# The mLSTM gates' eight columns, moved into the first memory query group

## The chip, the cores and the metric

The kernel runs on one core of a Trainium2 chip. The time is that of the device for one launch, in microseconds (us). Before the change it is 1012.1 us, the median of three runs (1011.96 to 1012.36). One further execution was recorded by the hardware profiler; every duration and start time below is from it.

The engines are TensorE (PE in the profile; PEld is its loading of stationary operands), VectorE (DVE), ScalarE (ACT), GpSimd (POOL) and SyncE (SP), whose queue issues the loads of weights. Each engine works through its own queue in order; semaphores tie the queues together.

## The reference, cut to what matters

The program is a decoder trunk of two layers for one sequence of 256 tokens with 1024 features. Layer 0 mixes tokens with an mLSTM, layer 1 with sliding-window attention; in both, four memory heads attend to 256 memory tokens. Each layer has a half-step SwiGLU feed-forward network before and after the mixing.

```python
hn = rms_norm(x, mix_norm_g[i])
proj = hn @ a_w_in[j]                       # 1024 x 3592
y_tok = mlstm_heads(proj[..., :A_TOK], a_gate_b[j], a_h_norm_g[j])
xq = proj[..., A_TOK:]                      # the 512 memory query columns
y_mem = memory_heads(xq, mem_k, mem_v, xa_q_norm_g[i], xa_k_norm_g[i])

# in mlstm_heads: q, k, v, the output gate, and then the eight gate columns
gates = tok[..., o4:].astype(f32) + gate_b.astype(f32)
i_pre = gates[..., :A_HEADS]                # 4 input gates
logf = jax.nn.log_sigmoid(gates[..., A_HEADS:])   # 4 forget gates
```

The forget gates are summed along the sequence, and a running maximum stabilises the exponentials. In the weight matrix, columns 3072 to 3079 are the gates, and columns 3080 to 3591 the memory queries: they lie next to each other.

## The kernel before, in words

All matrix products with weights are in fp32 split in two: a weight tile is loaded into `wr`, ScalarE casts it to a high part `wh` (L211), VectorE subtracts to get a low part `wl` (L212), and each product is three matmuls (`mm3`, L225 to L227): high by high, high by low, low by high. There are five `wr` buffers and eight of each of `wh` and `wl`, so the cast of a tile waits until TensorE is done with the tile eight before it. Activations are stored transposed (features in partitions) and split in `xh` and `xl` (L241), with the gain of the norm multiplied in; the norm's factor per token is applied to the products, as a row `rb` or as columns `rc`.

A `Group` (L316) makes 256 output columns: two weight tiles of four 128-row chunks, 24 matmuls each. With `rows=True` the activations are the stationary operand, and tokens come out in partitions; otherwise features do.

The order on TensorE and on SyncE's queue is the order in which the program emits the work. A small planner, `Weave`, decides that: one main chain emits groups, and side chains (`wv.spawn`) come in after a delay written in the table `LAT`, counted on a clock that the emitted matmuls advance. On VectorE, ScalarE and GpSimd the order is made when the program is built, by a scheduler; at run time they follow it strictly.

The mLSTM mixer (`mixer_a`, L649) emits in this order: four groups for the output gate (`g0`, `g1`, `g2` and a fourth); the gates; two groups of memory queries; groups for q and k; four groups for v; and the output projection. The gates before the change: the eight columns are loaded (L679) and put into columns 0 to 3 and 32 to 35 of a zeroed 128-column tile (L681 to L686), and eight `mm3` with this tile as stationary operand give the gates as rows in partitions 0 to 3 and 32 to 35 (L688 to L690). The gate chain on these rows (L693 to L708) is: copies out of PSUM, the product with `rb`, the bias, the log of a sigmoid (exp and ln on ScalarE), a sum scan, a maximum scan, and a last exp. The result `gg` is written to DRAM (L710), and read back twice, spread over all partitions, into `gb` (L713); both are issued from ScalarE's queue. 20 us after the gates on the planner's clock, `gate_cols` turns two of the rows into columns (`acol`).

`cross_spawn` (L568) handles a memory query group: `head_norm` (L368: square, sum, scaling, a power on GpSimd at L379, scaling, a product at L383), a side chain after `cross`, 9.5 us, that transposes the queries (`turn`, L387) and copies them out of PSUM to `qT` (L576, on ScalarE), and two heads, of which the first starts with the product of `qT` with `kT` (L588, recorded at L231). `scores` (L732) uses `gb` and `acol` for the mLSTM's own scores.

Of the kernel before, what the change touches and what calls it, by code (L numbers as in the profile page):

```python
# [10 lines left out]
F32 = mybir.dt.float32  # L11
# [8 lines left out]
P = 128  # L20
# [12 lines left out]
def constants():  # L33
# [17 lines left out]


LAT = dict(pieces=1, norm=7.5, norm_b=4.8, mnorm=2.4, x0=16.0, x0_b=7.5, mkeys=7.2, cross=9.5, cross_s=1.5,
           cross_m=3.7, cross_p=8.7, cross_o=3.0, gates=20.0, scores=2.2, scores_m=8.4, num=6.9, num_r=7.5,
           keys=5.5, keys_d=7.2, query=9.0, head=1.5, head_m=2.5, head_p=9.3, head_o=4.0)


# [41 lines left out]
def tile_trunk(ctx: ExitStack, tc: tile.TileContext, a, out):  # L99
# [31 lines left out]
    def act(*args, **kw):  # L131
        ins = nc.scalar.activation(*args, **kw)  # L132
        if args[2] not in (AF.Copy, AF.Square):
            tabled[0] = ins
# [232 lines left out]

    def head_norm(dst, src, n, hsc):  # L368

        hd = src.shape[2] // n  # L370
        sq, v, u = tmp(), col(), col()
        sqv = sq[:, :, :n * hd]
        act(sqv, src, AF.Square)
        nc.vector.tensor_reduce(out=v[:, 0:2 * n].rearrange("p (h m) -> p h m", h=2),
                                in_=sqv.rearrange("p h (m d) -> p h m d", m=n), axis=AX.X, op=ALU.add)
        for h in range(2):
            nc.vector.tensor_scalar(u[:, n * h:n * h + n], v[:, n * h:n * h + n], hsc[:, h:h + 1], EPS,
                                    op0=ALU.mult, op1=ALU.add)
        nc.gpsimd.tensor_tensor(out=u[:, 8:8 + 2 * n], in0=u[:, 0:2 * n], in1=mhalf[:, 0:2 * n], op=ALU.pow)  # L379
        for h in range(2):  # L380
            nc.vector.tensor_scalar(v[:, 8 + n * h:8 + n * h + n], u[:, 8 + n * h:8 + n * h + n],
                                    hsc[:, 2 + h:3 + h], None, op0=ALU.mult)
        tt(out=dst.rearrange("p h (m d) -> p h m d", m=n), in0=src.rearrange("p h (m d) -> p h m d", m=n),  # L383
           in1=v[:, 8:8 + 2 * n].rearrange("p (h m) -> p h m", h=2).unsqueeze(3).to_broadcast([P, 2, n, hd]),
           op=ALU.mult)
# [179 lines left out]
        def has(self, *kcs):  # L565
            return lambda: all(kc in self.done for kc in kcs)

    def cross_spawn(gr, gi, layer, hsc, ys):  # L568
        qn = unit(F32)
        head_norm(qn, gr.ps, 2, hsc)  # L570
        cell = []

        def queries():
            ps = turn(qn)
            qT = unit(F32)
            act(qT, ps, AF.Copy, scale=gqk[:, layer:layer + 1])  # L576
            cell.append(qT)
            for m in range(2):
                wv.spawn(head(m), LAT['cross_s'] + LAT['cross_m'] * m)
            return  # L580
            yield

        def head(m):
            hd, qT = gi * 2 + m, cell[0]
            hi, lo = ys.tiles(4 + gi)
            s = mo()
            for h in range(2):
                mmf(s[:, h * T:(h + 1) * T], qT[:, m, h * P:(h + 1) * P], kT[gi][:, m], T)  # L588
            sv = halves(s)
            c = col()  # L590
            nc.vector.tensor_reduce(out=c[:, 2:4], in_=sv, axis=AX.X, op=ALU.max, negate=True)  # L591
            p = unit(F32)
            for h in range(2):
                act(p[:, h], sv[:, h], AF.Exp, bias=c[:, 2 + h:3 + h], accum_out=c[:, 4 + h:5 + h])
            nc.vector.reciprocal(c[:, 6:8], c[:, 4:6])
            tt(out=p, in0=p, in1=c[:, 6:8].unsqueeze(2).to_broadcast([P, 2, T]), op=ALU.mult)
            yield LAT['cross_p']
            tps = mo()
            for mc in range(2):
                for h in range(2):  # L600
                    transpose(tps[:, mc * T + h * P:mc * T + (h + 1) * P], p[:, h, mc * P:(mc + 1) * P])
            pT = tmp()
            nc.scalar.copy(pT, halves(tps))
            yield LAT['cross_o']
            o = mo()
            for mc in range(2):
# [42 lines left out]
    def mixer_a(x, nxt):  # L649
# [25 lines left out]
        table("natural_log_exp_and_others")  # L675


        raw = mk(wrp, [P, 8, 8], F32, "wr")
        nc.sync.dma_start(raw, w.rearrange("(k p) f -> p k f", p=P)[:, :, 3072:3080])  # L679
        gh, gl = mk(whp, [P, 8, P], F32R, "wh"), mk(wlp, [P, 8, P], F32R, "wl")  # L680
        nc.vector.memset(gh.bitcast(F32), 0.0)  # L681
        nc.vector.memset(gl.bitcast(F32), 0.0)
        for s in range(2):
            src, dst = raw[:, :, s * 4:s * 4 + 4], slice(s * 32, s * 32 + 4)
            nc.scalar.copy(gh[:, :, dst], src)
            tt(out=gl[:, :, dst], in0=src, in1=gh[:, :, dst].bitcast(F32), op=ALU.subtract)  # L686
        ps = mo()
        for kc in range(8):  # L688
            mm3(ps[:, :T], gh[:, kc], gl[:, kc], x.xh[kc // 2][:, kc % 2], x.xl[kc // 2][:, kc % 2],
                start=kc == 0, stop=kc == 7)  # L690
        gt = [unit(F32) for _ in range(4)]
        ipre, fpre, ab, bc, av, gg, em, one = (gt[i // 2][0:4, i % 2] for i in range(8))
        nc.vector.memset(one, 1.0)  # L693
        nc.scalar.copy(ipre, ps[0:4, :T])
        nc.scalar.copy(fpre, ps[32:36, :T])
        tt(out=ipre, in0=ipre, in1=x.rb[0:4], op=ALU.mult)
        tt(out=fpre, in0=fpre, in1=x.rb[0:4], op=ALU.mult)
        nc.vector.tensor_scalar(ipre, ipre, gbias[:, 0:1], None, op0=ALU.add)
        nc.vector.tensor_scalar(fpre, fpre, gbias[:, 1:2], None, op0=ALU.add)
        nc.vector.scalar_tensor_tensor(out=ab, in0=fpre, scalar=-1.0, in1=fpre, op0=ALU.mult, op1=ALU.max)  # L700
        act(ab, ab, AF.Exp, scale=-1.0)
        act(ab, ab, AF.Ln, bias=1.0)
        nc.vector.scalar_tensor_tensor(out=fpre, in0=fpre, scalar=0.0, in1=ab, op0=ALU.min, op1=ALU.subtract)
        nc.vector.tensor_tensor_scan(bc, one, fpre, 0.0, ALU.mult, ALU.add)
        tt(out=av, in0=ipre, in1=bc, op=ALU.subtract)
        nc.vector.tensor_tensor_scan(gg, one, av, 0.0, ALU.mult, ALU.max)
        tt(out=em, in0=bc, in1=gg, op=ALU.add)
        act(em, em, AF.Exp, scale=-1.0)  # L708
        gd = a["gd"]
        nc.scalar.dma_start(gd, gg)  # L710
        gb = [unit(F32) for _ in range(2)]
        for i in range(2):
            nc.scalar.dma_start(gb[i], gd[2 * i:2 * i + 2, :].partition_broadcast(P))  # L713
        acol = mk(gp, [P, 16], F32, "acol")

        def gate_cols():
            pc = mo()
            for i, r in enumerate((av, em)):
                for h in range(2):
                    transpose(pc[:, (2 * i + h) * 4:(2 * i + h) * 4 + 4], r[:, h * P:(h + 1) * P])  # L720
            nc.vector.tensor_copy(acol, pc[:, :16])
            return
            yield

        wv.spawn(gate_cols(), LAT['gates'])
        hsc = head_scales(x.rc, P, True)
        for gi in range(2):
            gr = Group(w, 3080 + gi * 256, x.xh, x.xl, rows=True)
            yield from gr.all()
            cross_spawn(gr, gi, 0, hsc, ys)  # L730

        def scores(hd):  # L732
            row = gb[hd // 2][:, hd % 2]
            d = unit(F32).rearrange("p a b -> p (a b)")
            tt(out=d[:, :T], in0=maskd, in1=row, op=ALU.subtract)
            tt(out=d[:, T:384], in0=maskd[:, :P], in1=row[:, P:], op=ALU.subtract)
            act(d[:, :T], d[:, :T], AF.Exp, bias=acol[:, hd:hd + 1])
            act(d[:, T:384], d[:, T:384], AF.Exp, bias=acol[:, 4 + hd:5 + hd])
            q, k = qk[hd // 2][:, hd % 2], qk[2 + hd // 2][:, hd % 2]
            sps = mo()  # L740
            mmf(sps[:, :T], k[:, :P], q, T)
            mmf(sps[:, T:384], k[:, P:], q[:, P:], P)
            tt(out=d[:, :384], in0=d[:, :384], in1=sps[:, :384], op=ALU.mult)
            sd[hd] = d
            return
            yield

        for gi in (0, 2, 1, 3):
            gr = Group(w, gi * 256, x.xh, x.xl)
# [113 lines left out]
    def mixer_b(x, nxt):  # L863
# [26 lines left out]
                                  kn[:, :, :P].rearrange("p h (j d) -> p h j d", j=2))  # L890
        wv.spawn(keys(kdr, vr), LAT['keys'])
        hsx, hsq = head_scales(x.rc, P, True), head_scales(x.rc, 64, True)
        cross_spawn(g1, 0, 1, hsx, ys)
        gr = Group(w, 1280 + 256, x.xh, x.xl, rows=True)
        yield from gr.all()
        cross_spawn(gr, 1, 1, hsx, ys)

        def v22(x4):
            return x4.rearrange("p (h e) -> p h e", h=2)
# [127 lines left out]
```

## Time and profile before

| what | value |
|---|---|
| median of three runs | 1012.1 us (1011.96 to 1012.36) |
| the profiled execution | 1012.23 us |
| its span | 1010.4 us |
| TensorE busy | 998.5 us, 99% of the span |
| VectorE, ScalarE, GpSimd busy | 655.5, 519.5, 35.7 us |
| mean DMA rate | 181 GB/s |
| matmuls of the gates begin | 238.53 us |
| first memory group, second | 241.25 us, 246.69 us |
| first ScalarE copy of the gates (L694) | 242.51 us |
| write of `gg` to DRAM, issued | 249.36 us |
| first transpose of queries; first product with `kT` | 257.79 us, 260.96 us |

Times such as 242.51 us count from the start of the span. In a time line a row gives start, duration, engine, line, operation, what it writes and reads, and in brackets how long the engine was idle before and who ended that. Operations issued through helpers carry the helper's line: most ScalarE activations are L132. A matmul's duration overlaps the next; what one costs in a stream is the distance between starts.

### The profile page before, as it was taken

To read this page: it belongs to the slowest core of one execution; us is meant where nothing else is said; L and a number is where in the kernel's file an instruction comes from. 1 tells how busy PE (TensorE), PEld (TensorE's weight loads), DVE (VectorE), ACT (ScalarE), POOL (GpSimd) and SP (SyncE) were. 2 spreads that over 40 slices of the span, in tenths; PEclk is the share of its full clock that TensorE was granted. 3 is DMA by queue.
4 is the path that set the end of the run, shared out by engine and by line. 5 is a ranking of instruction groups with operands and counts; after the bars stand their busy time and mean duration, and the time that the engine had idled before them with its cause. 6 is when DMAs were issued, how large, how long until landed. Compare 5 with 4: busy or idle time off the path is not lost.

```text
span 1010.4 us, 20624 instructions
## 1 busy us (share of the span) xinstructions
PE 998.5 (99%) x8594; PEld 980.2 (97%) x8594; DVE 655.5 (65%) x1063; ACT 519.5 (51%) x764; POOL 35.7 (4%) x32
## 2 busy tenths in 40 slices
PE   8999999999999999999999999999999999999998
PEld 7999999999999999999999999999987899999998
DVE  6866665577856676665558666656787766666551
ACT  7754445446656554444445544544557754454440
POOL 1200000000001000000000000000121000000000
PEclk9999999999999999999999999999999999999999
DMA  9776656666644566665676666567541347666550
GB/s 308 242 245 200 192 180 185 199 183 179 184 139 133 167 210 195 200 189 170 192 206 205 189 191 201 173 197 198 182 131 66 100 131 220 198 189 185 188 170 21
DMA packets 173204, 182.70 MB, mean 181 GB/s; under 512 B 7124, under 2 KB 168328, under 8 KB 173112
## 3 DMA queue, kind: packets, MB, share of 16 engines
q1 hardware_dynamic: 171872, 179.60, 58.3%
q10 hardware_dynamic: 1016, 1.58, 0.5%
q8 instruction: 67, 1.10, 0.5%
q0 software_dynamic: 224, 0.22, 0.2%
q14 instruction: 25, 0.20, 0.1%
HBM read 180.32 MB, written 1.05 MB: 180 GB/s over the span
## 4 chain that ended last, share of the span: by engine, by line
PE 94%; DVE 3%; ACT 1%; DMA 1%; POOL 0%; issue 0%; SPq 0%; ACTq 0%
PE bank L225 30%; PE bank L226 30%; PE bank L227 30%; PE bank L231 2%; PE bank L236 1%; ACT u L132 1%; DVE wl L212 1%; DMA wr<-in_mem_w_kv_dram 1%; PE bank L961 1%; POOL col L379 0%; DVE col L930 0%; DVE u L383 0%; DVE col L591 0%; PE bank L925 0%; DVE u L946 0%
## 5 line engine op out<-in xcount | busy, mean ns | idle before, releaser
L212 DVE TENSOR_TENSOR wl<-wr,wh 128x1024 fp32r<-128x1024 f32 (+1 forms) x347 | 414.7, 1196 | 279.8 <-ACT wh L211 279.0
L211 ACT CAST wh<-wr 128x1024 fp32r<-128x1024 f32 (+1 forms) x347 | 356.8, 1031 | 393.1 <-PE bank L226 368.9
L225 PE MATMUL bank<-xh,wh 128*128 128x256 f32 x1544 | 429.1, 278 | 0.0
L226 PE MATMUL bank<-xl,wh 128*128 128x256 f32 x1544 | 426.8, 276 | 0.0
L227 PE MATMUL bank<-xh,wl 128*128 128x256 f32 x1544 | 426.8, 276 | 0.0
L226 PEld LDWEIGHTS bank<-xl,wh 128*128 128x128 f32 x1544 | 290.3, 188 | 0.1
L225 PEld LDWEIGHTS bank<-xh,wh 128*128 128x128 f32 x1544 | 290.0, 188 | 0.1
L227 PEld LDWEIGHTS bank<-xh,wl 128*128 128x128 f32 x1544 | 289.9, 188 | 0.0
L225 PE MATMUL bank<-u,wh 128*128 128x256 f32 x896 | 249.3, 278 | 0.0
L226 PE MATMUL bank<-u,wh 128*128 128x256 f32 x896 | 247.6, 276 | 0.0
L227 PE MATMUL bank<-u,wl 128*128 128x256 f32 x896 | 247.6, 276 | 0.0
L225 PEld LDWEIGHTS bank<-u,wh 128*128 128x128 f32 x896 | 168.2, 188 | 1.9 <-issue 1.7
L226 PEld LDWEIGHTS bank<-u,wh 128*128 128x128 f32 x896 | 168.4, 188 | 0.1
L227 PEld LDWEIGHTS bank<-u,wl 128*128 128x128 f32 x896 | 168.3, 188 | 0.0
L225 PE MATMUL bank<-wh,xh 128*128 128x256 f32 x208 | 59.7, 287 | 0.0
L226 PE MATMUL bank<-wl,xh 128*128 128x256 f32 x208 | 57.9, 278 | 0.0
L227 PE MATMUL bank<-wh,xl 128*128 128x256 f32 x208 | 57.9, 278 | 0.0
L476 DVE TENSOR_TENSOR t<-bank,rb 128x256 f32<-128x256 f32 x88 | 36.6, 420 | 7.3 <-PE bank L227 7.3
L225 PEld LDWEIGHTS bank<-wh,xh 128*128 128x128 f32 x208 | 39.1, 188 | 0.5 <-issue 0.3
L226 PEld LDWEIGHTS bank<-wl,xh 128*128 128x128 f32 x208 | 39.1, 188 | 0.1
L227 PEld LDWEIGHTS bank<-wh,xl 128*128 128x128 f32 x208 | 39.0, 187 | 0.0
L479 DVE TENSOR_TENSOR t<-t,bank 128x256 f32<-128x256 f32 x88 | 32.7, 412 | 1.8 <-ACT t L132 1.8
(171 smaller groups left out, 657.5 us busy)
## 6 DMA issues: line engine op xcount, KB each, us to landing
wr<-in_ffn_w_in_dram SPq DMA_DIRECT2D x176, 512.0 KB, 3.6
wr<-in_ffn_w_out_dram SPq DMA_DIRECT2D x80, 512.0 KB, 3.5
wr<-in_a_w_in_dram SPq DMA_DIRECT2D x28, 512.0 KB, 3.9
wr<-in_b_w_in_dram SPq DMA_DIRECT2D x14, 512.0 KB, 4.6
wr<-in_a_w_out_dram SPq DMA_DIRECT2D x12, 512.0 KB, 3.3
wr<-in_b_w_out_dram SPq DMA_DIRECT2D x12, 512.0 KB, 3.4
wr<-in_ffn_w_out_dram SPq DMA_DIRECT2D x16, 256.0 KB, 2.8
wr<-in_mem_w_kv_dram SPq DMA_DIRECT2D x7, 512.0 KB, 8.0
```

Source lines behind the costliest of these rows:

```text
L132: ins = nc.scalar.activation(*args, **kw)
L211: last[0] = nc.scalar.copy(hi[:, i * n:(i + 1) * n], src[:, i * n:(i + 1) * n])
L212: tt(out=lo[:, i * n:(i + 1) * n], in0=src[:, i * n:(i + 1) * n], in1=hi[:, i * n:(i + 1) * n].bitcast(F32), op=ALU.subtract)
L225: nc.tensor.matmul(ps, wh, xh, start=start, stop=False, skip_group_check=True)
L226: nc.tensor.matmul(ps, wh, xl, start=False, stop=False, skip_group_check=True)
L227: nc.tensor.matmul(ps, wl, xh, start=False, stop=stop, skip_group_check=True)
L231: nc.tensor.matmul(ps, lhsT, rhs, start=start, stop=stop, skip_group_check=True)
L236: nc.tensor.transpose(ps, src, ident[:k, :k])
L476: tt(out=t[:, m], in0=ps[m][:, :T], in1=x.rb, op=ALU.mult)
L479: tt(out=t[:, m], in0=t[:, m], in1=ps[m][:, T:], op=ALU.mult)
L961: nc.tensor.matmul(o[es[e], cs], vr[:, i, js], pTs[e][:, src], start=i == 0, stop=i == 1, skip_group_check=True)
```

## The change

The gates' eight columns and the first 256 memory query columns, neighbours in the weight matrix, are now one group of 264 columns. Its weights come in three tiles (3, 3 and 2 chunks of 128 rows, 264 columns wide), and the two halves of the tokens go to two PSUM banks. The gates come out with tokens in partitions; ScalarE scales them by `rc` into columns 0 to 3 and 32 to 35 of a zeroed buffer `gts`, and two transposes on TensorE turn them into the rows that the gate chain expects. The chain, now without the products with `rb`, and the DMAs of `gd` and `gb` are in a side chain `gates`, 1.8 us after the group on the planner's clock, and the transposes that make `acol` follow 13.5 us after that. `scores` puts itself off until `gated` is set. `head_norm` takes a list of two banks as well, and then does the square and the last product in halves.

```diff
-           ... gates=20.0, ...
+           ... gates=13.5, ... gate=1.8,
 def head_norm(dst, src, n, hsc):
...
+        if isinstance(src, list):
+            for h in range(2):
+                act(sqv[:, h], src[h], AF.Square)
...
+                tt(out=dst[:, h].rearrange("p (m d) -> p m d", m=n), in0=src[h].rearrange("p (m d) -> p m d", m=n),
+                   in1=v[:, 8 + n * h:8 + n * (h + 1)].unsqueeze(2).to_broadcast([P, n, hd]), op=ALU.mult)
...
-        raw = mk(wrp, [P, 8, 8], F32, "wr")
-        nc.sync.dma_start(raw, w.rearrange("(k p) f -> p k f", p=P)[:, :, 3072:3080])
-        gh, gl = mk(whp, [P, 8, P], F32R, "wh"), mk(wlp, [P, 8, P], F32R, "wl")
-        nc.vector.memset(gh.bitcast(F32), 0.0)
-        nc.vector.memset(gl.bitcast(F32), 0.0)
...
-        for kc in range(8):
-            mm3(ps[:, :T], gh[:, kc], gl[:, kc], x.xh[kc // 2][:, kc % 2], x.xl[kc // 2][:, kc % 2],
-                start=kc == 0, stop=kc == 7)
+        gts = unit(F32)[:, :, :36]
+        nc.vector.memset(gts, 0.0)
+        gps = [mo(), mo()]
+        for c0, nk in ((0, 3), (3, 3), (6, 2)):
+            wt = wtile(w.rearrange("(k p) f -> p k f", p=P)[:, c0:c0 + nk, 3072:3336], nk, 264)
+            for m in range(2):
+                ms = slice(m * P, (m + 1) * P)
+                for k in range(nk):
+                    kc = c0 + k
+                    mm3(gps[m][:, :264], x.xh[kc // 2][:, kc % 2, ms], x.xl[kc // 2][:, kc % 2, ms],
+                        wt[0][:, k], wt[1][:, k], start=kc == 0, stop=kc == 7)
+                yield
+        for h in range(2):
+            act(gts[:, h].rearrange("p (s c) -> p s c", c=4)[:, 0:9:8], gps[h][:, :8].rearrange("p (s c) -> p s c", s=2),
+                AF.Copy, scale=x.rc[:, h:h + 1])
...
-        tt(out=ipre, in0=ipre, in1=x.rb[0:4], op=ALU.mult)
-        tt(out=fpre, in0=fpre, in1=x.rb[0:4], op=ALU.mult)
...
+        gated = []
+
+        def gates():
+            ps = mo()
+            for h in range(2):
+                transpose(ps[:36, h * P:(h + 1) * P], gts[:, h])
...
+            nc.scalar.dma_start(gd, gg)
+            for i in range(2):
+                nc.scalar.dma_start(gb[i], gd[2 * i:2 * i + 2, :].partition_broadcast(P))
+            yield LAT['gates']
...
+            gated.append(True)
+
+        wv.spawn(gates(), LAT['gate'])
         hsc = head_scales(x.rc, P, True)
-        for gi in range(2):
-            gr = Group(w, 3080 + gi * 256, x.xh, x.xl, rows=True)
-            yield from gr.all()
-            cross_spawn(gr, gi, 0, hsc, ys)
+        cross_spawn([p[:, 8:264] for p in gps], 0, 0, hsc, ys)
+        gr = Group(w, 3080 + 256, x.xh, x.xl, rows=True)
+        yield from gr.all()
+        cross_spawn(gr.ps, 1, 0, hsc, ys)
 
         def scores(hd):
+            while not gated:
+                yield 1.0
```

More of the change, by code (lines that the diff above doesn't have):

```diff
@@ L53 @@
 LAT = dict(pieces=1, norm=7.5, norm_b=4.8, mnorm=2.4, x0=16.0, x0_b=7.5, mkeys=7.2, cross=9.5, cross_s=1.5,
-           cross_m=3.7, cross_p=8.7, cross_o=3.0, gates=20.0, scores=2.2, scores_m=8.4, num=6.9, num_r=7.5,
+           cross_m=3.7, cross_p=8.7, cross_o=3.0, gates=13.5, scores=2.2, scores_m=8.4, num=6.9, num_r=7.5, gate=1.8,
            keys=5.5, keys_d=7.2, query=9.0, head=1.5, head_m=2.5, head_p=9.3, head_o=4.0)
@@ L368, in head_norm @@
     def head_norm(dst, src, n, hsc):
-        hd = src.shape[2] // n
+        hd = dst.shape[2] // n
         sq, v, u = tmp(), col(), col()
         sqv = sq[:, :, :n * hd]
-        act(sqv, src, AF.Square)
+        if isinstance(src, list):
+            for h in range(2):
+                act(sqv[:, h], src[h], AF.Square)
+        else:
+            act(sqv, src, AF.Square)
         nc.vector.tensor_reduce(out=v[:, 0:2 * n].rearrange("p (h m) -> p h m", h=2),
@@ L382, in head_norm @@
                                     hsc[:, 2 + h:3 + h], None, op0=ALU.mult)
+        if isinstance(src, list):
+            for h in range(2):
+                tt(out=dst[:, h].rearrange("p (m d) -> p m d", m=n), in0=src[h].rearrange("p (m d) -> p m d", m=n),
+                   in1=v[:, 8 + n * h:8 + n * (h + 1)].unsqueeze(2).to_broadcast([P, n, hd]), op=ALU.mult)
+            return
         tt(out=dst.rearrange("p h (m d) -> p h m d", m=n), in0=src.rearrange("p h (m d) -> p h m d", m=n),
@@ L566, in has, with cross_spawn @@
             return lambda: all(kc in self.done for kc in kcs)
-    def cross_spawn(gr, gi, layer, hsc, ys):
+    def cross_spawn(ps, gi, layer, hsc, ys):
         qn = unit(F32)
-        head_norm(qn, gr.ps, 2, hsc)
+        head_norm(qn, ps, 2, hsc)
         cell = []
@@ L675, in mixer_a @@
         table("natural_log_exp_and_others")
-        raw = mk(wrp, [P, 8, 8], F32, "wr")
-        nc.sync.dma_start(raw, w.rearrange("(k p) f -> p k f", p=P)[:, :, 3072:3080])
-        gh, gl = mk(whp, [P, 8, P], F32R, "wh"), mk(wlp, [P, 8, P], F32R, "wl")
-        nc.vector.memset(gh.bitcast(F32), 0.0)
-        nc.vector.memset(gl.bitcast(F32), 0.0)
[L683 to L686, printed above, removed]
@@ L687, in mixer_a @@
-        ps = mo()
-        for kc in range(8):
-            mm3(ps[:, :T], gh[:, kc], gl[:, kc], x.xh[kc // 2][:, kc % 2], x.xl[kc // 2][:, kc % 2],
-                start=kc == 0, stop=kc == 7)
+        gts = unit(F32)[:, :, :36]
[10 more added lines that the diff above has]
+                yield
@@ L691, in mixer_a @@
+        for h in range(2):
+            act(gts[:, h].rearrange("p (s c) -> p s c", c=4)[:, 0:9:8], gps[h][:, :8].rearrange("p (s c) -> p s c", s=2),
+                AF.Copy, scale=x.rc[:, h:h + 1])
         gt = [unit(F32) for _ in range(4)]
         ipre, fpre, ab, bc, av, gg, em, one = (gt[i // 2][0:4, i % 2] for i in range(8))
-        nc.vector.memset(one, 1.0)
-        nc.scalar.copy(ipre, ps[0:4, :T])
-        nc.scalar.copy(fpre, ps[32:36, :T])
-        tt(out=ipre, in0=ipre, in1=x.rb[0:4], op=ALU.mult)
@@ L697, in mixer_a @@
-        tt(out=fpre, in0=fpre, in1=x.rb[0:4], op=ALU.mult)
[L698 to L708, printed above, removed]
         gd = a["gd"]
-        nc.scalar.dma_start(gd, gg)
         gb = [unit(F32) for _ in range(2)]
-        for i in range(2):
-            nc.scalar.dma_start(gb[i], gd[2 * i:2 * i + 2, :].partition_broadcast(P))
@@ L714, in mixer_a @@
         acol = mk(gp, [P, 16], F32, "acol")
-        def gate_cols():
+        gated = []
+        def gates():
+            ps = mo()
+            for h in range(2):
+                transpose(ps[:36, h * P:(h + 1) * P], gts[:, h])
+            nc.vector.memset(one, 1.0)
+            nc.scalar.copy(ipre, ps[0:4, :T])
+            nc.scalar.copy(fpre, ps[32:36, :T])
+            nc.vector.tensor_scalar(ipre, ipre, gbias[:, 0:1], None, op0=ALU.add)
+            nc.vector.tensor_scalar(fpre, fpre, gbias[:, 1:2], None, op0=ALU.add)
+            nc.vector.scalar_tensor_tensor(out=ab, in0=fpre, scalar=-1.0, in1=fpre, op0=ALU.mult, op1=ALU.max)
+            act(ab, ab, AF.Exp, scale=-1.0)
+            act(ab, ab, AF.Ln, bias=1.0)
+            nc.vector.scalar_tensor_tensor(out=fpre, in0=fpre, scalar=0.0, in1=ab, op0=ALU.min, op1=ALU.subtract)
+            nc.vector.tensor_tensor_scan(bc, one, fpre, 0.0, ALU.mult, ALU.add)
+            tt(out=av, in0=ipre, in1=bc, op=ALU.subtract)
+            nc.vector.tensor_tensor_scan(gg, one, av, 0.0, ALU.mult, ALU.max)
+            tt(out=em, in0=bc, in1=gg, op=ALU.add)
+            act(em, em, AF.Exp, scale=-1.0)
+            nc.scalar.dma_start(gd, gg)
+            for i in range(2):
+                nc.scalar.dma_start(gb[i], gd[2 * i:2 * i + 2, :].partition_broadcast(P))
+            yield LAT['gates']
@@ L721, in gate_cols @@
             nc.vector.tensor_copy(acol, pc[:, :16])
-            return
-            yield
-        wv.spawn(gate_cols(), LAT['gates'])
+            gated.append(True)
+        wv.spawn(gates(), LAT['gate'])
         hsc = head_scales(x.rc, P, True)
-        for gi in range(2):
-            gr = Group(w, 3080 + gi * 256, x.xh, x.xl, rows=True)
-            yield from gr.all()
-            cross_spawn(gr, gi, 0, hsc, ys)
+        cross_spawn([p[:, 8:264] for p in gps], 0, 0, hsc, ys)
+        gr = Group(w, 3080 + 256, x.xh, x.xl, rows=True)
+        yield from gr.all()
+        cross_spawn(gr.ps, 1, 0, hsc, ys)
         def scores(hd):
+            while not gated:
+                yield 1.0
             row = gb[hd // 2][:, hd % 2]
@@ L744, in scores @@
             sd[hd] = d
-            return
-            yield
         for gi in (0, 2, 1, 3):
@@ L892, in mixer_b @@
         hsx, hsq = head_scales(x.rc, P, True), head_scales(x.rc, 64, True)
-        cross_spawn(g1, 0, 1, hsx, ys)
+        cross_spawn(g1.ps, 0, 1, hsx, ys)
         gr = Group(w, 1280 + 256, x.xh, x.xl, rows=True)
         yield from gr.all()
-        cross_spawn(gr, 1, 1, hsx, ys)
+        cross_spawn(gr.ps, 1, 1, hsx, ys)
         def v22(x4):
```

## The prediction

> **What bounds the kernel now.** I read the page first, then a table of stretches around the mLSTM mixer's gates, then the time lines of TensorE, ScalarE and GpSimd there.
>
> ```profile
> span 1010.4 us, 20624 instructions
> PE 998.5 (99%) x8594; PEld 980.2 (97%) x8594; DVE 655.5 (65%) x1063; ACT 519.5 (51%) x764; POOL 35.7 (4%) x32
> ```
>
> ```profile
> 235.00:245.00 10.00, 10.00 (x91) 10.00 (x90) 6.57 (x10) 6.98 (x10) 0.00 (x0) 1.00 0.64 179
> 245.00:255.00 10.00, 10.00 (x90) 10.00 (x89) 8.95 (x20) 5.53 (x9) 1.91 (x1) 1.00 0.68 180
> 255.00:265.00 10.00, 10.00 (x83) 9.67 (x81) 7.79 (x14) 5.39 (x9) 1.91 (x1) 1.00 0.80 240
> ```
>
> Columns of the second: stretch, length, busy time of PE, PEld, DVE, ACT, POOL, granted clock, DMA share, GB/s. TensorE is without a gap here and the clock is 1.00: a matmul less is time less, one for one, and any wait put before a matmul is time more. VectorE is at 90% of the stretch in which the gates are made.
>
> ```profile
> 257.79 0.60 PE L236 MATMUL bank<-con,u 128*128 128x128 f32 x4
> ...
> 260.96 1.02 PE L231 MATMUL bank<-kT,u 128*128 128x256 f32 x4
> ```
>
> The first line is the transpose of the first memory queries, the second the scores product that needs them back as qT. Between them stand 24 matmuls of the next weight tile, and in that time ScalarE must do the copy L576:
>
> ```profile
> 249.36 0.51 ACTq L710 DMA_DIRECT2D gd_dram<-u  x1
> 249.92 0.42 ACT L132 ACTIVATE u<-u 4x256 f32<-4x256 f32 x1 [1.50 <-DVE col L377]
> 250.25 1.03 ACT L211 CAST wh<-wr 128x1024 fp32r<-128x1024 f32 x1
> 250.72 1.69 ACTq L713 DMA_DIRECT2D u<-gd_dram  x2
> 252.47 0.60 ACT L132 ACTIVATE t<-bank 128x512 f32<-128x512 f32 x1 [1.19 <-PE bank L227]
> ...
> 257.87 1.05 ACT L211 CAST wh<-wr 128x1024 fp32r<-128x1024 f32 x1 [1.77 <-PE bank L226]
> 258.82 0.68 ACT L132 ACTIVATE u<-bank,gqk 128x512 f32<-128x512 f32 x1
> ```
>
> Here gd is written to DRAM at 249.36; the loads that read it back wait for it and issue from 250.72 (1.36 later) to 252.41; the next ScalarE work starts at 252.47. So the loads hold ScalarE's queue. The copy comes long after, at 258.82, 2.1 us before it is needed.
>
> ```profile
> 250.00 1.91 POOL L379 TENSOR_TENSOR col<-col,mhalf 128x4 f32<-128x4 f32 x1 [24.59 <-DVE col L377]
> 255.10 1.91 POOL L379 TENSOR_TENSOR col<-col,mhalf 128x4 f32<-128x4 f32 x1 [3.19 <-DVE col L377]
> ...
> 727.76 1.01 POOL L379 TENSOR_TENSOR col<-col,mhalf 128x4 f32<-128x4 f32 x1 [4.19 <-DVE col L377]
> ```
>
> The power of a head norm takes GpSimd 1.91 us with a VectorE split (L212) beside it, 1.01 without.
>
> **The change on TensorE.** Removed: 24 matmuls. They start every 0.1133 us (241.25 to 252.13 is 96 of them), so −2.72. Added: 8 columns on 48 matmuls. A row crosses 256 columns already: 128x257 takes 380 ns, 128x256 382 to 388, so no step; by columns 0.1133×8/256×48 = +0.17 (ends 0 and that doubled). Added: two transposes to 36x128. The four 128x128 ones cost 0.44 us net, the 4x4 ones 0.10 each; I take the former, +0.22 (0.20 to 0.25). Sum −2.33.
>
> [...]
>
> **Off TensorE, costed at nothing.** Removed are two VectorE memsets (0.91 each), four small splits (0.28, 0.32) and two products with rb (0.41 each). Added are a small memset, two scaled ScalarE copies, and the square and the product of the first head norm in halves. The three loads of 264 columns take the place of a 32 KB and two 512 KB loads in SP's queue, three for three; landings are 3.8 and 3.9 us. The splits run eight weight tiles (about 21 us) ahead of TensorE, which covers all of it. One is nearer: the first 264-column cast and split now stand before the last xh/xl split (L241). ScalarE sat 2.26 us idle there (before 219.10); the cast waits for TensorE's first mixer tile (218.4) and ends about 219.25, so xl ends near 220.95 instead of 220.80. TensorE reads it at 221.8: no wait; bounds 0 and +0.3.
>
> **The gates, moved.** They now hang on the first memory group instead of going before it, and the order of the built kernel puts much in front of them. The groups start at 238.53 (241.25 − 24×0.1133). In the changed order:
> - TensorE: 48×0.1168 to 244.1; half the second group to 246.85; transposes of the gates to 247.1; query weights; transpose of qn at 255.3; the kT product would start at 258.5 to 258.6.
> - ScalarE: a cast waits for the tile that ends at 246.85, 247.05 to 248.0; the row copies L694 and L695 to 248.7; the second group's square 250.0 to 250.6.
> - VectorE: first norm's sum 245.3, its power 1.91 (a split runs beside it), scaling at 248.4, two products to 249.5, memset 0.3, a split 249.8 to 250.9, L698 to L700 to 252.0, the second norm's sum and L377 to 253.0. Its power waits with VectorE idle, so 1.01: scaling 254.1 to 254.4. A split to 255.5, L703 0.44, scan 0.7 to 256.6, a split to 257.7, L705, scan L706 and L707 (0.44+0.71+0.41) to 259.3.
> - ScalarE: exp and gd write at 259.3 (249.36 before). Loads of gb 1.37 later, 260.7, issuing for 1.69 to 262.4. **Only then** the qT copy, which the changed order puts behind them: 262.45 + 0.69 = 263.1. The kT product starts at 263.2.
>
> TensorE waits 263.2 − 258.55 = 4.65 us, its longest wait here, where it had none. Set against before: the product starts 263.2 − 260.96 = +2.24 later. What is late next: the second norm's product L383 ends at about 262.7, still before its transpose (263.2+0.86+1.36 = 265.4). Later work keeps its distances; gb lands 6 us after issue (268) and is read some 10 us behind that. While the loads of gb ran before (252.5 to 257.7) matmuls came every 0.1179 us, 0.2 in all; they run after the wait now, so up to +0.2 stays. I take +0.1. Sum: −2.33 + 4.65, or +2.3 with it, on the profiled run's own 1012.23 (its span 1010.4 + 1.8), which is 0.13 over the median: 1014.4 against 1012.1.
>
> Unknown: the second issue of gb.
>
> ```profile
> L713 ACTq DMA_DIRECT2D u<-gd_dram x2: 357/832/1307, 250.7 to 251.1; - x2
> ```
>
> One took 0.36, one 1.31. Taking both short gives +1.3, as seen +2.3; I take the row as it is, being the same pair. The VectorE chain of thirteen steps may be 1 us off either way: a power of 1.91 instead of 1.01 gives +0.9.
>
> **Rivals.** A change under 0.2% (2.02 us) can't be told from none.
> 1. The forecast, +1.3 to +3.2, 1013.4 to 1015.3: 60%, two thirds of it over +2.02.
> 2. The long wait lowers TensorE's clock. No gap over 1.5 us exists before and the clock is 1.00 in every stretch, so the trace can't show it. If the matmuls ran at half rate for as long as the wait, 4.65 us of wall would do half its work: +2.3 more, 1016.7. 20%.
> 3. The loads do not hold the copy (the 252.47 row also had its matmul at 252.3, so it speaks only by 0.15 us). Then L383 is the limit: the second transposes start at 262.8 where the pair stood at 263.33, −0.5: 1011.6. 12%.
> 4. The other side: the gate chain is out early enough. It needs exp at 254.6 instead of 259.3 and L383 by 260.6; then nothing waits and −2.33 stands, 1009.8, faster. For it: two products fewer, TensorE 2.3 ahead. Against: six splits and two norms between its steps in the changed order, and a chain that took 242.5 to 249.8 even when put first. 8%. That the removed matmuls do not save is excluded: nothing else ran out there.
>
> [...]
>
> **Numbers.** Likeliest 1014.4. Slower: 40 + 20 = 60%; within 0.2%: 20 + 12 = 32%; faster 8%. The range runs from rival 3 to rival 2 with half a microsecond over it, 1011.6 to 1017.2; it leaves out rival 4 and little else.
>
> **What would show it.** Right: a TensorE wait of 3.5 to 5.5 us before a kT product (L231's line), put down to ScalarE; gd written near 259 and the qT copy right behind two gb issues; the 264-column group at 0.117 a matmul; no wait at the first mixer tiles. Wrong: that product within a microsecond of 258.5; another wait in the gates' own transposes; a granted clock under 1.00 around 264.

## The result, and the profile after

The changed kernel takes 1017.5 us (median of four runs, 1016.6 to 1018.4), the kernel before 1012.1: **1.0053 times as long, interval 1.0036 to 1.007, or 5.4 us more**. The forecast was 1014.4 with a range to 1017.2. The direction was right; the loss is more than twice the forecast one, and the time lies outside the range. The profiled execution took 1016.86 us by itself, its span 1015.1 against 1010.4 before: 4.7 us are to be found in it.

One thing is needed to read the times below: in some executions TensorE's granted clock is also 0.50 for 3.41 us right after the thin opening of the program (within 13 to 18.1 us; from 14.56 to 17.97 in one profile), which moves every later start by 1.3 to 1.7 us; the profiles of before and after shown here are without it, while two of the changed kernel's four runs have it by their times and mean clocks (1018.1 and 1018.4 us, 0.995), so that without it the loss is 4.5 to 4.7 us.

The page's head, changed kernel:

```profile
span 1015.1 us, 20581 instructions
PE 999.3 (98%) x8572; PEld 980.4 (97%) x8572; DVE 653.7 (64%) x1060; ACT 520.1 (51%) x766; POOL 33.7 (3%) x32
```

There are 22 matmul records less, and yet TensorE's busy time has grown by 0.8 us: some matmuls have become longer. The table of stretches (length; busy time of PE, PEld, DVE, ACT, POOL; granted clock; DMA share; GB/s) shows which:

```profile
255.00:260.00 5.00, 4.02 (x36) 3.82 (x34) 4.90 (x8) 1.77 (x3) 0.00 (x0) 1.00 0.61 168
260.00:265.00 5.00, 2.12 (x6) 1.76 (x7) 2.66 (x6) 1.43 (x2) 0.00 (x0) 0.71 0.74 215
265.00:270.00 5.00, 5.00 (x26) 4.55 (x26) 1.72 (x4) 1.71 (x5) 0.00 (x0) 0.61 0.42 142
270.00:275.00 5.00, 5.00 (x42) 4.89 (x42) 3.86 (x7) 3.02 (x10) 0.00 (x0) 1.00 0.01 2
```

Between 255 and 265 TensorE stands idle for 3.9 us, where before it had no gap. Then, from 265 to 270, it is busy all the time, but with 26 matmuls where the next stretch has 42, at a clock of 0.61. The time line of TensorE has both, the wait and the slow matmuls:

```profile
255.68 0.60 PE L236 MATMUL bank<-con,u 128*128 128x128 f32 x4
...
258.74 0.28 PE L227 MATMUL bank<-xh,wl 128*128 128x256 f32 x1
262.88 2.08 PE L231 MATMUL bank<-kT,u 128*128 128x256 f32 x4 [3.87 <-ACT u L132]
264.40 0.78 PE L225 MATMUL bank<-xh,wh 128*128 128x256 f32 x1
264.97 0.42 PE L226 MATMUL bank<-xl,wh 128*128 128x256 f32 x1
265.19 0.42 PE L227 MATMUL bank<-xh,wl 128*128 128x256 f32 x1
```

The transpose of the first memory queries is 2.11 us earlier than before (257.79), the product with `kT` 1.92 later (260.96). Behind it, matmuls start every 0.21 us; ahead of it every 0.113. The transposes of the softmax that follow (`tps`) start at 274.88, against 270.11 before:

```profile
274.88 0.60 PE L236 MATMUL bank<-con,u 128*128 128x128 f32 x4
```

```profile
270.11 0.60 PE L236 MATMUL bank<-con,u 128*128 128x128 f32 x4
```

That is +4.77, and this distance stays (304.53 against 299.75 for the next products with `v`). So the account of this execution closes: **+1.92 up to the product and +2.85 behind it, where the clock is low.**

ScalarE's time line shows what the product waited for:

```profile
255.76 1.05 ACT L211 CAST wh<-wr 128x1024 fp32r<-128x1024 f32 x1 [1.32 <-PE bank L226]
259.07 0.42 ACT L132 ACTIVATE u<-u 4x256 f32<-4x256 f32 x1 [2.26 <-DVE u L727]
259.07 0.52 ACTq L729 DMA_DIRECT2D gd_dram<-u  x1
259.69 1.04 ACT L211 CAST wh<-wr 128x1024 fp32r<-128x1024 f32 x1 [0.21 <-issue]
261.26 0.83 ACTq L731 DMA_DIRECT2D u<-gd_dram  x2
262.14 0.69 ACT L132 ACTIVATE u<-bank,gqk 128x512 f32<-128x512 f32 x1 [1.40 <-DMA gd_dram<-u]
```

The last line is the copy to `qT`. Its input is ready at about 256.3; it stands in the queue behind the gates' last exp (which waits 2.26 us for VectorE) and behind the loads of `gb` (which wait for the write of `gd` to land, 2.19 us from its issue to theirs). And GpSimd, the two powers:

```profile
246.51 1.91 POOL L385 TENSOR_TENSOR col<-col,mhalf 128x4 f32<-128x4 f32 x1 [21.09 <-DVE col L383]
252.85 1.01 POOL L385 TENSOR_TENSOR col<-col,mhalf 128x4 f32<-128x4 f32 x1 [4.43 <-DVE col L383]
```

### The profile page after: what moved, and what is told of

Read it like the earlier page. It is cut to its first block, busy times and chain, and to the rows that moved or that the text cites. A ratio compares the mean times of both kernels' runs of the same rounds, so it can differ in the third digit from the quotient of the medians.

```text
span 1015.1 us, 20581 instructions
## 1 busy us (share of the span) xinstructions
PE 999.3 (98%) x8572; PEld 980.4 (97%) x8572; DVE 653.7 (64%) x1060; ACT 520.1 (51%) x766; POOL 33.7 (3%) x32
## 3 DMA queue, kind: packets, MB, share of 16 engines
q10 hardware_dynamic: 1016, 1.58, 0.5%
## 4 chain that ended last, share of the span: by engine, by line
PE 91%; DVE 4%; ACT 2%; DMA 1%; POOL 1%; issue 1%; SPq 0%; ACTq 0%; DVEq 0%; POOLq 0%
PE bank L225 29%; PE bank L226 29%; PE bank L227 29%; PE bank L231 2%; ACT u L132 1%; DVE wl L212 1%; PE bank L236 1%; POOL col L385 1%; DMA wr<-in_mem_w_kv_dram 1%; DVE u L961 0%; DVE col L945 0%; PE bank L976 0%; DVE u L394 0%; DMA gd_dram<-u 0%; ACT wh L211 0%
## 5 line engine op out<-in xcount | busy, mean ns | idle before, releaser
L225 PE MATMUL bank<-wh,xh 128*128 128x256 f32 (+1 forms) x208 | 60.0, 288 | 0.0
L226 PE MATMUL bank<-wl,xh 128*128 128x256 f32 (+1 forms) x208 | 58.1, 279 | 0.0
L227 PE MATMUL bank<-wh,xl 128*128 128x256 f32 (+1 forms) x208 | 58.0, 279 | 0.0
```

Source lines behind the costliest of these rows:

```text
L225: nc.tensor.matmul(ps, wh, xh, start=start, stop=False, skip_group_check=True)
L226: nc.tensor.matmul(ps, wh, xl, start=False, stop=False, skip_group_check=True)
L227: nc.tensor.matmul(ps, wl, xh, start=False, stop=stop, skip_group_check=True)
```

## The experiments

The theory after the result: the gates' chain comes out late; the wait costs about 1.9 us net, as forecast, and the wait then costs as much again or more by lowering the clock. Rivals: the slow matmuls have another cause (the DMAs of `gb` that now run beside them), or the new group of 264 columns itself is the dearer part.

### Filling the wait: the clock theory

Twenty matmuls on constants, whose result nobody reads, are put right before the first product with `kT`. TensorE is then busy for most of the wait; nothing else is changed.

```diff
         def head(m):
...
+            if layer == 0 and hd == 0:
+                fill = mo()
+                for _ in range(20):
+                    nc.tensor.matmul(fill[:, :384], identb, maskb[:, :384], start=True, stop=True, skip_group_check=True)
```

> The changed kernel, with 20 bf16 matmuls of 384 columns (about 3.3 us) put before the first product with kT, so that TensorE is busy while it waits; nothing reads their result. Theory (the long wait lowers the clock): the wait itself stays, the product still starts near 262.9 us, but the matmuls behind it come every 0.113 to 0.118 us instead of 0.215, the granted clock is 1.00 throughout, and the time falls by about 2.9 us to 1014 to 1014.7, with less spread between runs. Rival (the clock has nothing to do with the idle time, or the rest is lost elsewhere): 1016.6 to 1018.5 as with the changed kernel.

Measured: 1014.1 us (median of 12), 1.0015 times before, interval 1.0002 to 1.0028: 3.3 us less than the changed kernel, and about 2.6 less where neither has the low clock at the opening (nine of these runs, median 1014.1, against 1016.6 and 1016.9). The stretches of its profile (an execution with the low clock at the opening, so all starts are 1.5 us later):

```profile
260.00:262.50 2.50, 2.50 (x18) 1.64 (x18) 1.87 (x4) 1.46 (x2) 0.00 (x0) 1.00 0.82 212
262.50:265.00 2.50, 1.44 (x10) 0.72 (x8) 2.29 (x4) 0.69 (x1) 0.00 (x0) 1.00 0.78 238
265.00:270.00 5.00, 5.00 (x37) 4.61 (x38) 2.33 (x5) 1.73 (x6) 0.00 (x0) 1.00 0.64 200
```

```profile
264.87 1.13 PE L231 MATMUL bank<-kT,u 128*128 128x256 f32 x4 [1.06 <-ACT u L132]
```

The product is no earlier (264.87 less the 1.5 is 263.3, after has 262.88), but the clock is 1.00 throughout. The loads of `gb` still run beside the matmuls, so they aren't what slows them. More work on TensorE, and less time: the clock's part is shown, at about 2.6 us.

### The chain two steps later: the wait itself

The exp, the write of `gd` and the loads are put off by 10 us of the planner's clock, so that they stand behind the copy to `qT` in ScalarE's order. All else stays as in the changed kernel, but that the transposes for `acol` come one product with `kT` later on TensorE.

```diff
             tt(out=em, in0=bc, in1=gg, op=ALU.add)
+            yield 10.0
             act(em, em, AF.Exp, scale=-1.0)
...
-            yield LAT['gates']
+            yield LAT['gates'] - 10.0
```

> The changed kernel, with the last exp of the gate chain and the write and loads of gd emitted 10 us later on the planner's clock, behind the copy of qT in ScalarE's queue; TensorE's order is unchanged. Theory (the copy is held by the loads in front of it): no wait at the product with kT, L394 also comes earlier in VectorE's order, no clock drop, and the 2.1 us that TensorE gained up to the transpose at 255.68 us stay: about 1010.0. Rival (L394 is late as well and takes over): a wait of 1 to 2 us at the second transposes, 1011 to 1012. Rival (the wait has another cause): 1017.

Measured: 1010.2 us (median of 12), 0.998 times before, interval 0.9963 to 0.9997: **faster than both kernels**. ScalarE's time line (this profile, too, is 1.6 us late from the opening):

```profile
257.37 1.05 ACT L211 CAST wh<-wr 128x1024 fp32r<-128x1024 f32 x1 [1.32 <-PE bank L226]
258.32 0.69 ACT L132 ACTIVATE u<-bank,gqk 128x512 f32<-128x512 f32 x1
261.17 0.42 ACT L132 ACTIVATE u<-u 4x256 f32<-4x256 f32 x1 [2.16 <-DVE u L727]
261.17 0.51 ACTq L730 DMA_DIRECT2D gd_dram<-u  x1
261.79 1.05 ACT L211 CAST wh<-wr 128x1024 fp32r<-128x1024 f32 x1 [0.20 <-issue]
262.79 0.83 ACTq L732 DMA_DIRECT2D u<-gd_dram  x2
```

The exp runs at 261.17, or 259.6 without the opening: half a microsecond later than in the changed kernel. Only the order differs. The copy comes straight after the cast, the product at 260.47 (258.9 without the opening, forecast for an unhindered start 258.5 to 258.6), and TensorE has no gap there. What remains is the saving of the merged group: 1012.3 − 1010.2 = 2.1 us, which is the 2.11 of the transpose above. So the 264 columns are not dear; the order is.

### The other way to make room: the queries' side chain later

```diff
-        wv.spawn(queries(), LAT['cross'])
+        wv.spawn(queries(), LAT['cross'] + (5.0 if layer == 0 else 0.0))
```

> The changed kernel, with the memory heads' transposes and what follows them 5 us later on the planner's clock in layer 0, so that TensorE has more weight matmuls to do before it needs qT. The gate chain and its DMAs stay as they are. Theory: the copy of qT is as late as before (about 262) but is no longer the last thing TensorE needs; wait 0 to 1 us, 1010.0 to 1011. If instead the memory heads are then late for the output projection, a new wait there, 1012 or more. Rival (another cause): 1017.

Measured: 1012.4 us (median of 12), 0.9995 times before, interval 0.9978 to 1.0011. Apart from one of 1018.1, the times lie in two clusters, 1011.0 to 1011.4 with a mean clock of 0.999 to 1.00 and 1012.4 to 1012.9 with 0.998, of about equal number: the second is the low clock at the opening, which the profiled execution has. The profile has a small wait left:

```profile
264.15 1.13 PE L231 MATMUL bank<-kT,u 128*128 128x256 f32 x4 [0.67 <-ACT u L132]
```

TensorE gets other work to do while the chain runs, and most of the wait goes; this is a second repair by order alone, about 1 us worse than the first (1011.1 and 1010.1, the lower cluster of each; 1011.1 is 0.1 over what was expected here).

### Lateness without the merge

Here the kernel before keeps its padded gate group; only the chain on the gates' rows, from the copies out of PSUM to the loads of `gb`, becomes a side chain that starts 7 us later.

```diff
+        def gates():
+            nc.vector.memset(one, 1.0)
+            nc.scalar.copy(ipre, ps[0:4, :T])
...
+            yield 13.5
...
-        wv.spawn(gate_cols(), LAT['gates'])
+        wv.spawn(gates(), 7.0)
```

> The kernel before, with its padded gate group and all its matmuls, and only the gate chain (copies to the loads of gb) emitted 7 us later on the planner's clock, one and a half half-groups behind the first memory group as in the change. Theory (lateness alone makes the wait): a wait of 4 to 6 us at the product with kT, the clock drops behind it, and the time is 1018 to 1020.5, above the changed kernel by the matmuls that it still has. Rival (the wide group or its two banks make the loss): 1012.

Measured: 1019.5 us (median of 8), 1.0061 times before, interval 1.004 to 1.0081. ScalarE's time line, then the product with `kT` and the stretch behind it (this profile is 1.3 us late from the opening):

```profile
262.31 0.41 ACT L132 ACTIVATE u<-u 4x256 f32<-4x256 f32 x1 [2.10 <-DVE u L713]
262.31 0.52 ACTq L715 DMA_DIRECT2D gd_dram<-u  x1
262.94 1.04 ACT L211 CAST wh<-wr 128x1024 fp32r<-128x1024 f32 x1 [0.21 <-issue]
265.15 0.91 ACTq L717 DMA_DIRECT2D u<-gd_dram  x2
266.11 0.69 ACT L132 ACTIVATE u<-bank,gqk 128x512 f32<-128x512 f32 x1 [2.13 <-DMA gd_dram<-u]
```

```profile
266.85 1.85 PE L231 MATMUL bank<-kT,u 128*128 128x256 f32 x4 [4.44 <-ACT u L132]
```

```profile
265.00:270.00 5.00, 3.15 (x12) 2.82 (x13) 2.19 (x5) 1.23 (x4) 0.00 (x0) 0.71 0.85 223
```

The same picture, the same order (exp, `gd`, cast, `gb`, copy), a wait of 4.4 us and a lowered clock, without any column of the merge. Lateness alone makes the whole loss; the merge, 2.0 us less than this kernel, makes a part of it good.

### The loads off ScalarE's queue

```diff
-            nc.scalar.dma_start(gd, gg)
+            nc.gpsimd.dma_start(gd, gg)
             for i in range(2):
-                nc.scalar.dma_start(gb[i], ...)
+                nc.gpsimd.dma_start(gb[i], ...)
```

> The changed kernel with the write of gd and the two loads of gb issued from GpSimd's queue instead of ScalarE's; the exp stays in front of the copy of qT. Theory (the loads hold the copy, on top of the late exp): the copy starts right behind the exp at 259.07 us and one cast, near 260.4, the product near 261.1, the gap is 2.3 us instead of 4.1, the clock stays at 1.00, and the time is 1012.0 to 1012.6. Rival (the loads do not hold the queue, the late exp and VectorE alone do): the product still near 262.9, 1017.

Measured: 1014.1 us (median of 10, 1012.3 to 1015.8), 1.0016 times before, interval 1.0007 to 1.0026. ScalarE and TensorE in its profile (no low clock at the opening):

```profile
258.87 0.42 ACT L132 ACTIVATE u<-u 4x256 f32<-4x256 f32 x1 [2.25 <-DVE u L727]
259.19 1.03 ACT L211 CAST wh<-wr 128x1024 fp32r<-128x1024 f32 x1
260.13 0.67 ACT L132 ACTIVATE u<-bank,gqk 128x512 f32<-128x512 f32 x1
```

```profile
260.86 1.28 PE L231 MATMUL bank<-kT,u 128*128 128x256 f32 x4 [2.03 <-ACT u L132]
```

The copy no longer waits for a DMA, and the wait before the product is 2.03 us instead of 3.87: **the loads held the queue for 1.8 us** (the product starts 2.0 us earlier, at 260.86 instead of 262.88, but this whole execution is 0.2 us earlier: its first transposes of queries are at 255.49, not 255.68). The other 2.0 us of the wait are the exp's, which waits for VectorE and has the copy behind it. But the expected clock of 1.00 did not come: the stretch from 260 to 265 has 0.67, after a gap of only 2.0 us. Three of the ten runs came to 1012.3 to 1012.5 with a mean clock of 1.00, the other seven to 1013.9 and more with 0.997 or 0.998. This part of the expectation failed for most runs, and led to the next ones.

### How long must a gap be?

With eight filling matmuls instead of twenty, the wait lies between the 1.06 us that left the clock alone and the 3.87 us that lowered it. (The expectations count from start to start: 2.3 and 2.9 us there are 2.0 and 2.6 us of idle time here.)

> The changed kernel with 8 filling matmuls (about 1.3 us) at the head of the 4.1 us gap, so that TensorE idles some 2.8 us in front of the product with kT instead of 4.1. Theory (the clock drops where the idle stretch is long enough, and some 1.4 us isn't): if 2.8 us is still short enough, the matmuls behind come at 0.113 to 0.118 us and the time is 1014.1 as with 20; if it is not, the clock drops as in the changed kernel and the time is 1017. Rival (the loss behind the gap grows in proportion to the idle time): about 2 us lost behind it, 1016.

> The changed kernel itself again, for comparison on the same chip: 1016.6 to 1018.5, product with kT near 262.9 us, half clock behind it.

Measured: eight fillers 1015.96 us (four runs, 1015.85 to 1018.0), 1.004 times before, interval 1.0025 to 1.0055; the changed kernel again 1017.4 (1.0045, interval 1.0028 to 1.0062), with a wait of 3.94 us and a clock of 0.76 and 0.56 behind it, so its loss repeats. The eight fillers' 1016 is what the rival in the expectation gives, but the profiled execution has the low clock at the opening, and none behind the wait. Its stretches:

```profile
260.00:265.00 5.00, 2.40 (x17) 1.56 (x16) 4.28 (x7) 2.15 (x3) 0.00 (x0) 1.00 0.79 214
265.00:270.00 5.00, 5.00 (x39) 4.63 (x38) 2.33 (x5) 1.97 (x6) 0.00 (x0) 1.00 0.75 214
```

A wait of 2.6 us left the clock at 1.00, one of 2.0 us lowered it. The gap's length alone doesn't decide it. Four more profiles, of these same two kernels:

> The kernel of e6_pool once more, for its profile alone: the same 2.3 us gap before the first kT product (261 us, or 1.6 later with a slow opening). If the length of the gap decides whether the clock falls, the clock behind it falls again as in e6_pool (0.6 to 0.8 in the stretch 260 to 265, matmuls 0.21 us apart) in each profile. If it is where the gap falls against something that runs by itself, the same gap is followed by a clock of 1.00 in some executions: the time is then near 1012.4 with an undisturbed opening, 1014.0 with a slow one.

> As for e8_pool_again: a third profile of the 2.3 us gap. By the gap's length: a lowered clock behind it again. By the moment of the gap: 1.00 or lowered, differing between the three profiles.

> The kernel of e5_fill8 once more, for its profile alone: a gap of 2.9 us that was followed by a clock of 1.00 in e5_fill8. By the gap's length alone it would be 1.00 again (and 2.3 us could not lower it in e6_pool either, so that theory then stands against itself). By the moment of the gap: lowered in some of the profiles, the time then some 1.6 to 2.2 us above what the opening alone explains (1014.3, or 1015.9 with a slow opening).

> As for e10_fill8_again: a third profile of the 2.9 us gap. By the gap's length: a clock of 1.00 behind it again. By the moment of the gap: it differs between the three profiles.

The stretches 260 to 265 and 265 to 270 of the kernel with the loads on GpSimd, its second profile and then its third:

```profile
260.00:265.00 5.00, 2.96 (x17) 2.66 (x17) 4.68 (x8) 2.18 (x4) 1.68 (x3) 0.87 0.79 215
265.00:270.00 5.00, 5.00 (x32) 4.52 (x32) 1.63 (x4) 2.19 (x8) 0.00 (x0) 0.79 0.70 211
```

```profile
260.00:265.00 5.00, 4.02 (x28) 3.66 (x29) 3.72 (x9) 2.53 (x7) 1.10 (x2) 1.00 0.79 179
265.00:270.00 5.00, 5.00 (x41) 4.87 (x40) 3.79 (x8) 2.98 (x9) 0.00 (x0) 1.00 0.56 182
```

The same program, the same wait (2.04 and 2.03 us), and once the clock falls and once it doesn't. All profiles together, where the fourth column, from the start of the product to the start of the softmax's transposes, gives the clock's price whatever the opening did:

| profile | wait | clock behind it | product to transposes | low at opening | time |
|---|---|---|---|---|---|
| before | none | 1.00 | 9.15 us | no | 1012.2 |
| twenty fillers | 1.06 us | 1.00 | 9.20 | yes | 1016.2 |
| loads on GpSimd, first | 2.03 | 0.67 | 10.85 | no | 1013.9 |
| second | 2.04 | 0.87, 0.79 | 10.81 | yes | 1015.7 |
| third | 2.03 | 1.00 | 9.24 | no | 1012.5 |
| eight fillers, first | 2.60 | 1.00 | 9.23 | yes | 1015.9 |
| second | 2.52 | 1.00 | 9.21 | no | 1013.9 |
| third | 2.34 | 1.00 | 9.20 | no | 1014.1 |
| changed kernel | 3.87 | 0.71, 0.61 | 12.00 | no | 1016.9 |
| changed kernel again | 3.94 | 0.76, 0.56 | 11.65 | yes | 1018.2 |
| lateness alone | 4.44 | 0.71, 0.95 | 10.83 | yes | 1019.8 |

A wait of 2.0 us lowers the clock in some executions (two of three profiles; by time and mean clock eight of twelve executions), waits of about 4 us did in all three profiles, and the price goes from 1.6 to 2.85 us. Of the six executions with eight fillers one, 1018.0 us with a mean clock of 0.997, looks as if the clock fell there too; it was not profiled.

How the wait stands against the clock's changes can be read from these traces, where the granted clock is either 1.00 or 0.50. In every profile all its changes stand whole steps of 3.413 us apart: the changed kernel has it low from 262.08 to 268.91, two steps; the second profile of the loads on GpSimd from 14.56 to 17.97 and from 263.73 to 267.14, one step each, with 72 between them. Where the steps stand differs from execution to execution. Here are the steps that hold the wait, second profile and then third (in which the steps are counted back from the clock's fall behind the last instruction):

```profile
260.32:263.73 3.41, 1.37 (x9) 1.07 (x8) 3.41 (x6) 1.93 (x3) 0.58 (x1) 1.00 0.73 179
263.73:267.14 3.41, 3.41 (x19) 3.08 (x17) 0.98 (x2) 1.08 (x5) 1.10 (x2) 0.50 0.72 194
```

```profile
256.43:259.84 3.41, 2.52 (x23) 2.32 (x21) 3.34 (x5) 1.16 (x3) 0.58 (x1) 1.00 0.86 225
259.84:263.25 3.41, 2.27 (x16) 2.17 (x16) 3.26 (x6) 1.21 (x3) 1.07 (x2) 1.00 0.79 231
```

In the second profile the whole wait lies in one step (3.41 less 1.37 busy, 2.04 idle), and the next step is at 0.50. In the third it is split, 0.89 and 1.14 us, and the clock stays at 1.00. All profiles of the table go this way: behind the wait the clock fell where one step held 2.03 us of idle time or more (2.03, 2.04, 2.17, 3.07, 3.15), and it stayed where the wait was split, with eight fillers into 1.20 and 1.40, 0.66 and 1.86, 0.88 and 1.46. So in these profiles the moment of the wait decided along with its length. The low clock lasted one step, or two where the wait reached into the first of them (the changed kernel, 0.80 and 1.78 us). In these few profiles 1.86 us of the wait in one step was the most without a fall, 2.03 the least with one.

## Why the prediction was wrong, and where it was right

**The failing step is rival 2, the wait that lowers TensorE's clock, left out of the likeliest sum at 20%.** It was named with its place, its price (+2.3) and its sum (1016.7), and a clock under 1.00 around 264 was among the signs of being wrong; the run had 0.71 there, +2.85 and 1016.86 in the profiled execution. That the median lies outside the range, though 1016.86 does not, is the low clock at the opening in two of the four runs, of which the prediction had no term. The price came out near by partial luck: it was worked out from half rate for as long as the wait, a supposition of the author's (the stretches of before have a clock of 1.00); the runs showed 0.50 in steps of 3.41 us, one costing 1.6 to 1.7 us and two 2.5 to 2.85. What stood against it, no gap over 1.5 us in the trace before, only said that the trace could not show it, not that it would not be. All eight runs of the changed kernel have a mean clock of 0.995 to 0.998. The 20% was the author's estimate too. By what was measured here (steps of 3.413 us, and a fall in each profile with 2.03 us or more of idle time in one) rival 2 was all but certain, again an estimate: however 4.65 us is split between two steps, one has 2.3 or more.

The rest of the likeliest case stands nearly step by step:

- **TensorE, −2.33:** −2.11 at the transpose. The term mis-sized is the group of 264: a matmul cost 0.121 us (from 238.54 to 244.35, 48 of them) where 0.1168 was taken, 0.2 us more in all. That is either +0.37 for the columns, over the bound of +0.34, or +0.15 for them and +0.22 for a slower pace of all matmuls there (0.1178 where 0.1133 was taken, as in the stretch right behind); the runs do not separate the two.
- **Off TensorE at nothing:** right; there is no new wait at the first mixer tiles, and the waits of the other places on TensorE are those of before to 0.2 us.
- **The chain to the exp:** forecast 259.3, run 259.07. The row copies began at 248.37 (forecast 248.0), the second power took 1.01 us, as taken, with VectorE idle beside it.
- **The loads of `gb` and the copy:** forecast 260.7 with 1.69 of issue and the copy at 262.45; run 261.26 with 0.83 and 262.14. Both sizes were off, and in opposite directions: the write of `gd` to the loads took 2.19 us, not 1.37, and neither issue of the pair was long:

```profile
L731 ACTq DMA_DIRECT2D u<-gd_dram x2: 357/402/446, 261.3 to 261.6; - x2
```

- **The wait, 4.65:** 4.14 from the start before it (258.74) to its own (262.88), 4.03 without the usual 0.11, listed as 3.87. **Net +2.24:** +1.92. The profiles of eight fillers without the low clock at the opening, 1013.9 and 1014.1 us, have the product where the changed kernel has it (262.65 and 262.70) and the clock at 1.00: they give the likeliest case as it was forecast, 1014.4, to half a microsecond.
- **Rival 3** (the loads do not hold the copy) is false: taking them off the queue made the wait 1.8 us shorter. It also missed a step: even then the exp stands before the copy and costs 2.0 us, so its 1011.6 would have been 1012.5, the third profile above.
- **Rival 4** (nothing waits, 1009.8) is what the kernel with the later exp does: 1010.2. The condition put on it, an exp by 254.6, was needlessly strict: the exp may be later if it only stands behind the copy.

## What to carry to other kernels

A chain moved later takes with it what stands behind it in each engine's order: look for the first instruction on the critical path that is queued behind the moved ones, and put these behind it; here that turned +5.4 us into −2.1. The wait on a busy TensorE cost its own length here and then, where 2.0 us or more of it fell into one step of 3.41 us, 1.6 to 2.9 us more by the clock (waits of 3.87 to 4.44 us did each time): put that into the likeliest sum and not into a rival, and where a wait can't be removed, matmuls that nobody needs are cheap in it: twenty of them took about 2.6 us off here.

## What was not expected of the hardware

**A clock lowered with no gap of a microsecond.** The opening of the program has TensorE at 37 to 53% of the time between 11 and 13 us, with gaps of 0.3 to 0.7 and of 0.9 us, and behind it the clock is low for one step in seven of the thirteen profiles. The changed kernel has both, 1.00 the first time and 0.57 and 0.79 again, so it is not the program. The stretches of the profile before, and of the twenty fillers:

```profile
13.00:16.00 3.00, 2.74 (x23) 2.74 (x24) 3.00 (x6) 2.70 (x4) 0.00 (x0) 1.00 1.08 387
16.00:18.00 2.00, 2.00 (x20) 2.00 (x19) 1.84 (x3) 2.00 (x4) 0.00 (x0) 1.00 1.08 403
```

```profile
13.00:16.00 3.00, 2.71 (x18) 2.72 (x19) 2.98 (x6) 2.67 (x4) 0.00 (x0) 0.78 1.09 388
16.00:18.00 2.00, 2.00 (x11) 2.00 (x11) 1.86 (x3) 2.00 (x4) 0.00 (x0) 0.50 1.07 401
```

20 matmuls against 11 in the same two microseconds. In the seven, the step ahead of the fall held 1.28 to 1.56 us of idle time, in five of the others no step there more than 1.07, but in one 1.31: the clock fell with less idle time here than behind the wait, where 1.86 us left it at 1.00, and why stays open. The kernel before was never profiled with it, but its times have two clusters, 1011.5 to 1012.5 us with a mean clock of 0.999 or 1.00 and 1013.6 to 1014.0 with 0.997 or 0.998, beside one of 1020.1 that stays unexplained.

**Two paces of the same matmul.** At a clock of 1.00, matmuls of 256 columns start every 0.1133 us in some stretches and every 0.1178 in others. The forecast put 0.1179 down to the loads of `gb` (252.5 to 257.7 before). In the changed kernel there are no such loads between 244.4 and 250.6, and that stretch has 0.1178, while 250.7 to 255.6 has 0.1133: so the loads are not the cause. What is stays open.

**The way through DRAM.** The same write and the same pair of loads took 1.36, 2.19 and 2.84 us from the issue of the one to the issue of the others (before, after, and with lateness alone), and 1.69, 0.83 and 0.91 us to issue.
